# Weight blocks of a hybrid encoder layer, split two blocks ahead of their use instead of one

## The chip, the cores and the metric

The kernel runs on one core of one Trainium2 chip. The metric is device time in microseconds (us) of one execution, as the median of 3 runs. The core has a matrix engine (TensorE, PE in the profile; its weight loads are listed apart as PEld), a vector engine (VectorE, DVE), a scalar engine (ScalarE, ACT), a general engine (GpSimd, POOL) and SyncE (SP), which here only issues DMAs. GpSimd issues DMAs too, in order with its own computations.

## The reference

One layer on 1024 tokens with 16 meta tokens ahead of them (L = 1040), D = 1024, all in float32:

```python
u = rms_norm(h, norm1_g) @ w_in                # w_in: 1024 x (mLSTM x, o, gates | q, k, v | two branch gates)
xc = silu(depthwise_conv(u.mx) + conv_b)       # per head: q_m, k_m = xc @ wq, xc @ wk;  v_m = u.mx
h_m = mlstm_bidirectional(q_m, k_m, v_m, gates)        # 4 heads, chunkwise recurrence, both directions
y_a = sigmoid(u.mo) * (rms_norm(h_m) * g + skip * xc)
y_b = neighbourhood_attention(rms_norm(u.q), rms_norm(u.k), u.v, rpb, meta_bias)   # 8 heads, 8x16 windows
mix = sigmoid(u.ga) * (y_a @ w_branch_a) + sigmoid(u.gb) * (y_b @ w_branch_b)
h = h + mix @ w_out
h = h + square(relu(rms_norm(h, norm2_g) @ w_ff1)) @ w_ff2
return h[:, 16:]
```

## The kernel before

**Products in three terms.** Nearly every large product is formed in a reduced-precision float type (`float32r`) in three terms: both factors are split into a high part and a low part (the rest), and high x high, high x low and low x high are summed in PSUM. `mm3` issues the three matmuls.

**Weight blocks.** `w_in` is cut into blocks of 128 output columns (128 x 1024 elements, 512 KB). 42 of them, and then the 8 blocks of `w_b` (128 x 512), go through one queue W, an instance of `Weights`, in the order of their use, which a table FILL sets: xm (input of the recurrence, blocks x), tmo (its output gate, m), q, k and v of the attention (n, v), the branch gates gb and ga (b, a). For block j, `high_to` takes a tile wh, and GpSimd's queue issues a DMA from `w_in` that rounds to the high part on its way (L161). `split_to` takes a tile wl, ACT writes the negated high part into it, and a second DMA from `w_in`, again on GpSimd's queue, adds the whole weight on top, which leaves the low part (L174):

```python
    def split_to(self, i):
        while self.n_lo <= min(i, len(self.srcs) - 1):
            self.high_to(j + 1)
            ...
            self.neg(l[:, 0:w], h[:, 0:w])
            self.nc.gpsimd.dma_start(l[:, 0:w], src, accum_op=OP.add)
```

A job that starts on block i calls `W.get(i)`, which splits up to block i + ahead. So with ahead = 1, when block i begins, the split of block i + 1 and the load of the high part of block i + 2 are asked for.

**g blocks.** `gemm_in` multiplies a weight block with the 8 normalised and split tiles of the input (xh, xl), in 2 or 3 blocks of columns; each is 24 matmuls into one of two PSUM banks (`gbank`, tile g), and then an evacuation by ACT or DVE (for gb, ACT's tanh). `gemm_in` is a generator, so that other work can go between its matmuls.

**What sets the order.** A `Filler` F holds these jobs. The recurrence of the four heads (`head_a` prepares q, k, v, the gates and masks of a head; `head_b` runs the 8 steps, forward and backward) is a chain of small matmuls (pi, pu, pn, 258 columns) between copies on ACT (nn, the state's high part Ch) and work on DVE. At points in it `F.share` puts in a share of the g matmuls. The next head's convolved inputs xc are split into xch and xcl at the end of the step loop (xcl by the same pair of negation and accumulating DMA, L239) and read by the matmuls pq. After the heads, the attention tiles are filled in the same way, then comes a stage of `w_b` (its g blocks are evacuated on DVE into gbq), beside which DVE and GpSimd form sums (ys, yq) for the products with the later weights, which the profile has from 850 us on. The instructions so written are ordered once more by a scheduler with its own model of time, engine by engine.

**Slots.** Weights, inputs, intermediate rows and masks share one pool of 44 tiles in SBUF, 128 x 1040 floats each (`slot`, NSLOT = 44). A tile is given out when its former user's last reader is done. Order on an engine and the giving of slots are fixed when the program is built.

Of the kernel before, what the change touches and what calls it, by code (L numbers as in the profile page):

```python
# [20 lines left out]
KC = 8  # L21
# [120 lines left out]
class Weights:  # L142
# [32 lines left out]
            self.parts[j][1] = l  # L175
            self.n_lo += 1

    def get(self, i, ahead=1):
        self.split_to(i + ahead)
        return self.parts.pop(i)  # L180


def build(tc, A, taps=None):
# [18 lines left out]
    def slot(name, dt=F32):  # L202
        return sp.tile([128, L], dt, name=name, tag="S")
# [16 lines left out]
    def copy(out, src, psum=False):  # L220
        n = free(out)
        k = load.pick([("V", 65 + n * (1.1 if psum else 0.55)), ("S", 90 + n * 0.85)])[0]
        if k == "V":
            V.tensor_copy(out, src)
        else:
            SC.copy(out, src)
# [99 lines left out]
    xh = [slot(f"xh{k}", F32R) for k in range(KC)]  # L326
    xl = [slot(f"xl{k}", F32R) for k in range(KC)]
# [71 lines left out]
    def gemm_block(wh, wl, n0, n, ks=KC, act=(xh, xl), off=0):  # L399
        ps = gbank()[:, 0:n]  # L400
        m = slice(n0 - off, n0 - off + n)
        for k in range(ks):
            c = slice(k * 128, (k + 1) * 128)
            mm3(ps, wh[:, c], wl[:, c], act[0][k][:, m], act[1][k][:, m], k == 0, k == ks - 1)
            yield 3 * n * 0.000422
        return ps
# [10 lines left out]
            ins = PE.matmul(ps, wl[:, k * 128:(k + 1) * 128], xh[k][:, m], start=False, stop=k == KC - 1)  # L417
        return ps, ins

    def gemm_in(wi, blocks, evac, ks=KC, act=(xh, xl), off=0, ahead=1):  # L420
        wh, wl = W.get(wi, ahead)
        for b, (n0, n) in enumerate(blocks):
            ps = yield from gemm_block(wh, wl, n0, n, ks, act, off)
            evac(b, n0, n, ps)
# [10 lines left out]
    def job_xm(j):  # L435
        xm[j] = slot(f"xm{j}")
        yield from gemm_in(w_mx[j], NB3, lambda b, n0, n, ps: copy(xm[j][:, n0:n0 + n], ps, True))
# [3 lines left out]
    def job_mo(j):  # L441
        tmo[j] = slot(f"tmo{j}")
        yield from gemm_in(w_mo[j], NB2, lambda b, n0, n, ps: SC.activation(
            tmo[j][:, n0 - NM:n0 - NM + n], ps, AF.Tanh, scale=0.5))
# [401 lines left out]
    def job_na(u):  # L846
        qf = slot(f"nqf{u}")
        yield from gemm_in(w_q[u], NB2, lambda b, n0, n, ps: copy(qf[:, n0 - NM:n0 - NM + n], ps, True),
                           ahead=1)
        kf = slot(f"nkf{u}")  # L850
        yield from gemm_in(w_k[u], NB3, lambda b, n0, n, ps: copy(kf[:, n0:n0 + n], ps, True),
                           ahead=1)
        NAT[u] = (qf, kf)

    def split_v(ps, out):
# [207 lines left out]
    def add_jobs(u):  # L1063
        for kind, j in FILL[u]:
            if kind == "x":
                F.add(f"xm{j}", job_xm(j), GX)
            elif kind == "m":
                F.add(f"mo{j}", job_mo(j), GE)
            elif kind == "b":
                F.add(f"gb{j}", job_gb(j), GE)  # L1070
            elif kind == "a":
                F.add(f"ga{j}", job_ga(j), GE)
            elif kind == "n":
                F.add(f"na{j}", job_na(j), GE + GX)
            else:
                F.add(f"nb{j}", job_nb(j), GX + 6)
# [655 lines left out]
```

## Time and profile before

| | before |
|---|---|
| median of 3 runs | 1669.43 us (1667.87 to 1671.40) |
| profiled execution | 1671.44 us, span 1669.7 us, mean granted clock 0.986 |
| PE / PEld / DVE busy | 1605.0 / 1358.5 / 1192.2 us (96% / 81% / 71%) |
| ACT / GpSimd busy | 806.1 / 420.8 us (48% / 25%) |

The span is the time from the first to the last instruction of the profiled execution; the rest of its time lies around it. The granted clock is the TensorE clock as a share of its full level (1.2 and 2.4 GHz are its two levels). Busy time of matmuls overlaps from one to the next: a 512-column matmul is recorded with 0.39 us, and the next begins 0.23 us after it. A number in square brackets at the end of a row is the idle time of the engine ahead of it in us, with what ended it. An operation is shown as out<-in by the names of the tiles; most instructions have line L137, the helper that records every operation, so they are told apart by their tiles.

### The profile page before, as it was taken

The numbers are of one execution on the slowest core, as the hardware profiler recorded it, in microseconds if no ns is written. First come the engines' busy times: TensorE is split into PE (matmuls) and PEld (weight loads), VectorE is DVE, ScalarE is ACT, GpSimd is POOL, SyncE is SP. The second block draws the span as 40 slices with busy tenths as digits, with TensorE's granted clock in tenths as the row PEclk, the third lists the DMA queues.
The fourth block names the chain that finished last, engine by engine and source line by source line (L and its number), as shares of the span: only waits on it lengthen the run. The fifth ranks groups of instructions, "written<-read, shape, count | busy, mean of one in ns | idle before, by whom it ended". The sixth has DMA issues, their size and how long they took to land.

```text
span 1669.7 us, 22510 instructions
## 1 busy us (share of the span) xinstructions
PE 1605.0 (96%) x8081; PEld 1358.5 (81%) x8081; DVE 1192.2 (71%) x2171; ACT 806.1 (48%) x1425; POOL 420.8 (25%) x476
## 2 busy tenths in 40 slices
PE   7998899999999999999899889799999999999999
PEld 7878789888989998888678667588888887888887
DVE  4537657474757776872589998986667685869597
ACT  5567566566747586753232335322222237353450
POOL 5010212122233313212466665640000000010100
PEclk9999999999999999999999999899999999999999
DMA  4352745546274534446735221033223558282833
GB/s 165 74 133 64 193 114 139 115 112 154 47 183 89 119 71 102 99 98 192 240 115 212 104 84 56 29 148 114 102 101 126 206 159 272 56 264 58 232 78 100
DMA packets 76399, 213.73 MB, mean 128 GB/s; under 512 B 11112, under 2 KB 21736, under 8 KB 76288
## 3 DMA queue, kind: packets, MB, share of 16 engines
q1 hardware_dynamic: 54976, 138.76, 23.7%
q0 software_dynamic: 21312, 73.54, 21.2%
q8 instruction: 64, 1.05, 0.3%
q14 instruction: 47, 0.39, 0.1%
HBM read 164.97 MB, written 38.76 MB: 122 GB/s over the span
## 4 chain that ended last, share of the span: by engine, by line
PE 71%; DVE 10%; issue 7%; DMA 7%; ACT 3%; POOL 2%; SPq 0%; POOLq 0%; DVEq 0%; ACTq 0%
PE pf L137 38%; PE g L137 23%; DMA wl<-w_in 3%; DVE ga L137 2%; PE po L137 2%; PE pp L137 1%; PE pt L137 1%; PE ps L137 1%; PE pi L137 1%; PE pn L137 1%; DMA gbd<-gbq 1%; PE pu L137 1%; DMA xcl<-xc 1%; DMA ra<-masks 1%; DMA wl<-w_b 1%
## 5 line engine op out<-in xcount | busy, mean ns | idle before, releaser
L137 PE MATMUL g<-xh,wh 128*128 128x512 f32 (+3 forms) x784 | 290.2, 370 | 7.4 <-DVE xm L137 3.9
L137 PE MATMUL g<-xh,wl 128*128 128x512 f32 (+3 forms) x784 | 287.6, 367 | 9.1 <-DMA wl<-w_in 9.1
L137 PE MATMUL g<-xl,wh 128*128 128x512 f32 (+3 forms) x784 | 286.9, 366 | 0.0
L137 PEld LDWEIGHTS g<-xh,wl 128*128 128x128 f32 x784 | 148.6, 190 | 28.8 <-DMA wl<-w_in 10.7
L137 PEld LDWEIGHTS g<-xh,wh 128*128 128x128 f32 x784 | 148.8, 190 | 25.7 <-DVE xm L137 4.2
L137 PEld LDWEIGHTS g<-xl,wh 128*128 128x128 f32 x784 | 148.8, 190 | 17.0
L137 DVE TENSOR_TENSOR acc<-acc,pf 128x512 f32<-128x512 f32 x96 | 64.0, 680 | 39.6 <-PE pf L137 34.6
L174 POOL DMA_DIRECT2D wl<-w_in x42 | 38.5, 917 | 140.6 <-ACT wl L137 75.5
L137 DVE CUSTOM_DVE_ANT_0 P<-ps,bt 128x400 f32<-128x400 f32 x64 | 36.0, 570 | 42.2 <-PE pp L137 22.3
L137 ACT COPY pu<-pf 128x512 f32<-128x512 f32 x20 | 11.7, 585 | 105.6 <-PE pf L137 105.6
L137 ACT ACTIVATE wl<-wh 128x1024 fp32r<-128x1024 f32 (+1 forms) x50 | 49.3, 988 | 26.5 <-PE g L137 12.7
L137 DVE SCALAR_TENSOR_TENSOR C<-C,decb,pu 128x258 f32<-128x258 f32 x52 | 23.6, 478 | 40.9 <-PE pu L137 40.6
L137 DVE SCALAR_TENSOR_TENSOR zq<-zq 128x512 f32<-128x512 f32 x64 | 47.4, 742 | 0.6
L137 ACT ACTIVATE P<-P,mn 128x400 f32<-128x400 f32 x64 | 40.3, 630 | 11.3 <-DVE mn L137 10.8
L137 DVE TENSOR_TENSOR pu<-pf,pu 128x512 f32<-128x512 f32 x40 | 27.3, 683 | 21.0 <-PE pf L137 21.0
L137 DVE TENSOR_TENSOR zq<-pf,pu 128x512 f32<-128x512 f32 x32 | 21.9, 684 | 25.4 <-PE pf L137 25.4
L161 POOL DMA_DIRECT2D wh<-w_in x42 | 28.0, 668 | 45.0 <-PE pk L137 14.5
L137 DVE TENSOR_SCALAR P<-P,sm 128x384 f32<-128x384 f32 (+1 forms) x128 | 38.4, 363 | 0.9
L137 DVE TENSOR_TENSOR zq<-pf,sp 128x512 f32<-128x512 f32 x32 | 21.9, 685 | 22.6 <-PE pf L137 22.4
L137 DVE TENSOR_TENSOR ptl<-pp,pth 128x384 fp32r<-128x384 f32 x64 | 35.5, 554 | 2.8 <-ACT pth L137 2.1
L137 ACT CAST pth<-pp 128x512 fp32r<-128x512 f32 x60 | 34.0, 581 | 5.4 <-PE pp L137 5.2
L137 POOL COPY bt<-mbias 128x32 f32<-128x32 f32 x32 | 8.3, 260 | 111.9 <-DVE mn L137 111.8
(2414 smaller groups left out, 4989.8 us busy)
## 6 DMA issues: line engine op xcount, KB each, us to landing
wh<-w_in POOLq DMA_DIRECT2D x42, 512.0 KB, 5.6
wl<-w_in POOLq DMA_DIRECT2D x42, 512.0 KB, 5.6
z2d<-zq SPq DMA_DIRECT2D x32, 512.0 KB, 3.7
zr<-z2d SPq DMA_DIRECT2D x32, 512.0 KB, 5.0
w2r<-w_ff SPq DMA_DIRECT2D x32, 512.0 KB, 13.0
bt<-rpbd SPq DMA_DIRECT2D x256, 32.0 KB, 2.8
xcl<-xc POOLq DMA_DIRECT2D x8, 520.0 KB, 5.0
ra<-rowd SPq DMA_DIRECT2D x8, 512.0 KB, 4.2
```

What stands on the lines that cost most here:

```text
L137: return fn(out, *a, **k)
L161: self.nc.gpsimd.dma_start(h[:, 0:src.shape[-1]], src)
L174: self.nc.gpsimd.dma_start(l[:, 0:w], src, accum_op=OP.add)
```

## The change

`ahead` is 2 instead of 1, in `Weights.get`, in `gemm_in` and in the two calls of `job_na`. When block i begins, the split of block i + 2 and the load of the high part of block i + 3 are asked for.

```diff
-    def get(self, i, ahead=1):
+    def get(self, i, ahead=2):
         self.split_to(i + ahead)
         return self.parts.pop(i)
...
-    def gemm_in(wi, blocks, evac, ks=KC, act=(xh, xl), off=0, ahead=1):
+    def gemm_in(wi, blocks, evac, ks=KC, act=(xh, xl), off=0, ahead=2):
         wh, wl = W.get(wi, ahead)
...
         yield from gemm_in(w_q[u], NB2, lambda b, n0, n, ps: copy(qf[:, n0 - NM:n0 - NM + n], ps, True),
-                           ahead=1)
+                           ahead=2)
...
         yield from gemm_in(w_k[u], NB3, lambda b, n0, n, ps: copy(kf[:, n0:n0 + n], ps, True),
-                           ahead=1)
+                           ahead=2)
```

Every engine has the same instructions as before; the order differs, nearly all of it in the stretch of the weight blocks. The numbers behind a tile's name count the tiles as the program takes them, the digits in the name are its own index.

On GpSimd's queue at the end of head 0 and the start of head 1: wl7 is the low part of block 7 of W, wh8 and wh9 the high parts of blocks 8 and 9, rv and rsh finish a head, kl1 is the low part of head 1's k, ra are the mask rows. Before:

```order
L137 TENSOR_SCALAR rv_1742<-ssh_1268 128x2 [waits Activation_49]
L137 TENSOR_TENSOR rsh_1269<-rv_1742,mhalf_108 128x2 [waits Pool_49]
L137 TENSOR_SCALAR rv_1745<-ssh_1268 128x2 [waits Activation_49]
L137 TENSOR_TENSOR rsh_1269<-rv_1745,mhalf_108 128x2 [waits Pool_49]
L137 TENSOR_SCALAR rv_1882<-ssh_1268 128x2 [waits DVE_49,Activation_49]
L137 TENSOR_TENSOR rsh_1269<-rv_1882,mhalf_108 128x2 [waits Pool_49]
L137 TENSOR_SCALAR rv_1885<-ssh_1268 128x2 [waits DVE_49,Activation_49]
L137 TENSOR_TENSOR rsh_1269<-rv_1885,mhalf_108 128x2 [waits Pool_49]
L161 DMA wh8_2123<-w_in 128x1024 [waits DMASW6_49,PE_49]
L239 DMA kl1_2096<-kf1_2032 128x1040 [waits DMASW7_49,DMASW2_49,Activation_49]
L651 DMA ra10_2100<-masks 128x1024 [waits DMAHW2_49,DMASW0_49]
L174 DMA wl7_2125<-w_in 128x1024 [waits DMASW1_49,Activation_49]
```

And after:

```order
L137 TENSOR_TENSOR rsh_1274<-rv_1747,mhalf_108 128x2 [waits Pool_49]
L174 DMA wl7_1926<-w_in 128x1024 [waits DMASW7_49,Activation_49]
L137 TENSOR_SCALAR mbias_706<-mbias_706 128x128
L137 TENSOR_SCALAR rv_1750<-ssh_1273 128x2 [waits Activation_49]
L137 TENSOR_TENSOR rsh_1274<-rv_1750,mhalf_108 128x2 [waits Pool_49]
L137 TENSOR_SCALAR rv_1887<-ssh_1273 128x2 [waits DVE_49,Activation_49]
L137 TENSOR_TENSOR rsh_1274<-rv_1887,mhalf_108 128x2 [waits Pool_49]
L137 TENSOR_SCALAR rv_1890<-ssh_1273 128x2 [waits DVE_49,Activation_49]
L137 TENSOR_TENSOR rsh_1274<-rv_1890,mhalf_108 128x2 [waits Pool_49]
L161 DMA wh9_2128<-w_in 128x1024 [waits DMASW0_49,DVE_49,PE_49]
L239 DMA kl1_2101<-kf1_2037 128x1040 [waits DMASW6_49,DMASW1_49,Activation_49]
L651 DMA ra10_2105<-masks 128x1024 [waits DMAHW5_49,DMAHW3_49,DMASW2_49]
```

The accumulation of wl7 has gone from behind the mask load ra10 to ahead of mbias and of most of the 128x2 operations; the loads of wh are one block further on.

On ACT at the end of head 2: gb3 is the fourth gate tile, evacuated in two halves, nn and Ch belong to the steps of the recurrence, xch7 and xcl7 are the next head's convolved input. Before:

```order
L137 ACTIVATE xt7_4059<-xc7_4055 128x1040
L137 ACTIVATE gb3_3952<-g_3958 128x512
L137 ACTIVATE jk_3962,ssh_3452<-ht20_3432 128x256
L137 ACTIVATE jk_3964,ssh_3452<-ht20_3432 128x256
L137 ACTIVATE nn_4016<-pi_3980,tm_699 128x258
L137 CAST Ch_3998<-C_3996 128x258
L137 ACTIVATE nn_4018<-pi_3984,tm_699 128x258
L137 ACTIVATE jk_3966,ssh_3452<-ht21_3433 128x256
L137 CAST Ch_4004<-C_4002 128x258
L137 CAST xch7_4135<-xc7_4055 128x1040
L137 ACTIVATE xcl7_4136<-xc7_4055 128x1040
L137 ACTIVATE gb3_3952<-g_4101 128x512
```

And after:

```order
L137 CAST Ch_4009<-C_4007 128x258
L137 ACTIVATE nn_4021<-pi_3985,tm_699 128x258
L137 ACTIVATE nn_4023<-pi_3989,tm_699 128x258
L137 ACTIVATE jk_3971,ssh_3457<-ht21_3438 128x256
L137 ACTIVATE jk_3973,ssh_3457<-ht21_3438 128x256
L137 ACTIVATE nn_4083<-pi_4067,tm_699 128x258
L137 ACTIVATE nn_4085<-pi_4071,tm_699 128x258
L137 ACTIVATE xt7_4064<-xc7_4060 128x1040
L137 ACTIVATE gb3_3957<-g_3963 128x512
L137 ACTIVATE gb3_3957<-g_4106 128x512
L137 CAST xch7_4140<-xc7_4060 128x1040
L137 ACTIVATE xcl7_4141<-xc7_4060 128x1040
```

The two evacuations of gb3 were ten rows apart; now they stand together, behind the nn of the following step and xt7. The pair of gb1 at the end of head 1 has moved in the same way, to behind two nn and two Ch. On TensorE, 18 small matmuls of the recurrence now stand between gb1's second g block and the next g block, and 46 between gb3's and the next; before it was none in both places.

On DVE in the w_b stage: gbq20 to gbq31 are evacuations of g blocks of `w_b`, ys and yq the sums. Before:

```order
L137 TENSOR_TENSOR yq10_9203<-yq00_9158,yq10_9203 128x1024
L137 SCALAR_TENSOR_TENSOR gbq20_9166<-gbq20_9166,g_9304 128x512
L137 TENSOR_TENSOR ys11_9335<-yq11_9205,yq13_9209 128x1024
L137 SCALAR_TENSOR_TENSOR gbq21_9168<-gbq21_9168,g_9319 128x512
L137 TENSOR_TENSOR yq11_9205<-yq01_9160,yq11_9205 128x1024
L137 TENSOR_TENSOR yq02_9162<-yq02_9162,yq00_9158 128x1024
L137 TENSOR_TENSOR ys11l_9343<-ys11_9335,ys11h_9342 128x1024
L137 SCALAR_TENSOR_TENSOR gbq30_9254<-gbq30_9254,g_9349 128x512
L137 SCALAR_TENSOR_TENSOR gbq31_9256<-gbq31_9256,g_9363 128x512
L137 TENSOR_TENSOR ys20l_9380<-yq00_9158,ys20h_9379 128x1024
```

And after:

```order
L137 SCALAR_TENSOR_TENSOR gbq20_9171<-gbq20_9171,g_9307 128x512
L137 TENSOR_TENSOR ys10_9337<-yq10_9208,yq12_9212 128x1024
L137 TENSOR_TENSOR yq10_9208<-yq00_9163,yq10_9208 128x1024
L137 SCALAR_TENSOR_TENSOR gbq21_9173<-gbq21_9173,g_9322 128x512
L137 TENSOR_TENSOR ys11_9338<-yq11_9210,yq13_9214 128x1024
L137 TENSOR_TENSOR yq11_9210<-yq01_9165,yq11_9210 128x1024
L137 SCALAR_TENSOR_TENSOR gbq30_9259<-gbq30_9259,g_9349 128x512
L137 TENSOR_TENSOR ys11l_9346<-ys11_9338,ys11h_9345 128x1024
L137 TENSOR_TENSOR yq02_9167<-yq02_9167,yq00_9163 128x1024
L137 SCALAR_TENSOR_TENSOR gbq31_9261<-gbq31_9261,g_9363 128x512
L137 TENSOR_TENSOR ys20l_9380<-yq00_9163,ys20h_9379 128x1024
L137 SCALAR_TENSOR_TENSOR gbq30_9259<-gbq30_9259,g_9397 128x512
```

The evacuation into gbq30 stood behind yq02 and ys11l and now stands ahead of both; gbq31 stays behind them.

## Rows read from the trace of the kernel before

**Rows 1.** Totals of the page, busy us, share and count per engine.

```profile
PE 1605.0 (96%) x8081; PEld 1358.5 (81%) x8081; DVE 1192.2 (71%) x2171; ACT 806.1 (48%) x1425; POOL 420.8 (25%) x476
```

**Rows 2.** Stages: stretch, length, PE, PEld, DVE, ACT, POOL (count), clock, DMA, GB/s.

```profile
57.00:300.00 243.00, 225.72 (x1333) 202.41 (x1332) 148.94 (x402) 149.22 (x316) 38.88 (x56) 0.98 0.51 122
300.00:757.00 457.00, 451.19 (x2639) 405.35 (x2639) 319.23 (x900) 302.96 (x626) 111.33 (x217) 1.00 0.46 105
757.00:850.00 93.00, 86.50 (x365) 67.55 (x363) 45.49 (x46) 32.61 (x46) 39.06 (x29) 0.96 0.71 216
850.00:1000.00 150.00, 139.63 (x567) 109.75 (x566) 140.10 (x128) 49.19 (x68) 99.76 (x53) 0.95 0.35 125
```

**Rows 3.** Matmuls reading tile wl: min/median/max ns, first to last start, forms.

```profile
L137 PE MATMUL g<-xh,wl x784: 276/390/665, 57.8 to 787.0; 128*128 128x512 f32 x112, 128*128 128x256 f32 x28, 128*128 128x384 f32 x28, 128*128 128x400 f32 x28
```

**Rows 4.** Waits of PE, 57 to 757 us: releaser, sum us, count, longest.

```profile
PE g L137 <- DMA wl<-w_in: 9.1, 5, 3.9
...
PE pi L137 <- ACT Ch L137: 3.3, 4, 2.1
```

**Rows 5.** Waits of PE, 757 to 850 us.

```profile
PE g L137 <- DVE gbq L137: 6.0, 5, 3.1
```

**Rows 6.** Timeline, 170 to 208 us: start, us, engine, line, operation.

```profile
170.58 0.29 POOL L137 TENSOR_SCALAR mbias<-mbias 128x128 f32<-128x128 f32 x1
...
190.11 1.05 ACT L137 ACTIVATE wl<-wh 128x1024 fp32r<-128x1024 f32 x1
...
192.27 1.15 POOL L174 DMA_DIRECT2D wl<-w_in  x1
...
207.39 0.50 PE L137 MATMUL g<-xh,wl 128*128 128x512 f32 x1 [3.88 <-DMA wl<-w_in]
```

**Rows 7.** DMA issues, 185 to 212 us: count, KB each, us to landing.

```profile
wl<-w_in POOLq DMA_DIRECT2D x1, 512.0 KB, 15.1
```

**Rows 8.** DMA issues over the whole span, page part 6.

```profile
wl<-w_in POOLq DMA_DIRECT2D x42, 512.0 KB, 5.6
```

**Rows 9.** A stretch behind 207 us, columns as in group 2.

```profile
208.00:212.00 4.00, 4.00 (x12) 3.16 (x11) 1.03 (x4) 1.86 (x7) 0.00 (x0) 0.58 0.90 317
```

**Rows 10.** Timeline, GpSimd's queue.

```profile
187.65 0.62 POOL L161 DMA_DIRECT2D wh<-w_in  x1 [7.34 <-PE pk L137]
```

**Rows 11.** Timeline, end of head 2.

```profile
357.22 0.92 POOL L239 DMA_DIRECT2D xcl<-xc  x1 [3.42 <-DVE ht L137]
...
360.04 0.48 ACT L137 ACTIVATE nn<-pi,tm 128x258 f32<-128x258 f32 x1 [0.23 <-PE pi L137]
...
370.92 0.39 PE L137 MATMUL pq<-xcl,wqk 128*128 128x512 f32 x1
```

**Rows 12.** Timeline, end of head 1, PE and ACT.

```profile
254.18 0.40 PE L137 MATMUL g<-xh,wh 128*128 128x512 f32 x1
...
259.05 0.40 ACT L137 CAST Ch<-C 128x258 fp32r<-128x258 f32 x1
```

**Rows 13.** Timeline, PE before 355 us.

```profile
353.80 0.28 PE L137 MATMUL pn<-vh,sml 128*128 128x258 f32 x1
...
353.92 0.39 PE L137 MATMUL g<-xh,wh 128*128 128x512 f32 x1
...
354.61 0.39 PE L137 MATMUL g<-xh,wh 128*128 128x512 f32 x1
```

**Rows 14.** Timeline, w_b stage.

```profile
818.76 1.22 DVE L137 TENSOR_TENSOR ys<-yq,yq 128x1024 f32<-128x1024 f32 x1
...
828.86 3.22 POOL L137 TENSOR_TENSOR yq<-ys,yq 128x1024 f32<-128x1024 f32 x1 [2.96 <-DVE yq L137]
...
829.77 3.38 DVE L137 TENSOR_TENSOR ys11l<-ys,ys11h 128x1024 fp32r<-128x1024 f32 x1
...
833.08 1.27 DVE L137 SCALAR_TENSOR_TENSOR gbq<-gbq,g 128x512 f32<-128x512 f32 x2
...
833.81 0.79 PE L137 MATMUL g<-yb0h,wh 128*128 128x512 f32 x1 [3.12 <-DVE gbq L137]
```

## The prediction

> **What bounds the kernel now.** I read the totals first [rows 1]. TensorE (PE) is busy 1605.0 of 1669.7 us; its weight loads, 81%, overlap its matmuls, and VectorE (DVE) has 71%, ScalarE (ACT) 48%, GpSimd 25%. The table by stage [rows 2] says where PE is not full. The weight blocks are used from 57.8 us [rows 3] to about 850. In that time, 57 to 300 us has PE busy 225.72 of 243.00 (17.3 free), 300 to 757 has 451.19 of 457.00 (5.8 free), and 757 to 850 has 86.50 of 93.00 (6.5 free). So the change can win little more than 29.6 us, under 2%, and only where its own wait is the one that ends last. From 850 to 1000 the busiest engine is DVE, 140.10 of 150.00.
>
> The list of PE's waits over the first two of these stages [rows 4] has the change's target in its first line: matmuls that read a low part wl wait for its landing 5 times, 9.1 us in all, the longest 3.9. The next line is of another kind, the rows pi of the recurrence that wait for ACT's copy of its state Ch. In the w_b stage [rows 5] the largest wait, 6.0 us, is for gbq, DVE's evacuation of PSUM, and not for a weight.
>
> **What the change does, step by step.** *The lead.* A block of w_in lasts (787.0 - 57.8) / 42 = 17.4 us on average [rows 3], so high and low parts are asked for about that much earlier. The longest wait shows that this is enough. The negated copy of that block stood on ACT at 190.11, and GpSimd issued its accumulating DMA at 192.27; PE took the block at 207.39 after 3.88 idle [rows 6]. That DMA took 15.1 us to land [rows 7], where the median of all 42 is 5.6 [rows 8]: two loads of masks went out around it. In the changed order on GpSimd's queue the same DMA (wl7) stands ahead of mbias, which ran at 170.58 [rows 6]. So it is issued at about 170, and even with 15.1 us it lands some 20 us before 207. The other four waits are 5.2 us together, each far shorter than a block. Term A: -9.1 us, bounds 0 (another input is late at the same places) and -9.1.
>
> *The clock.* After that 3.88 us wait the granted clock fell: 0.58 over 208 to 212 us, with 12 matmuls [rows 9]. At 0.23 us from one 512-column matmul to the next at the full level (three in 0.69 [rows 13]), 4 us hold 17.4; the 5.4 that are missing are 1.2 us. Without the wait this stretch should stay at the full level. Term B: -1.2, bounds 0 and -1.2.
>
> *The work.* Nothing is added: 50 negations on ACT, 50 copies and 50 accumulations on GpSimd's queue stay, each only earlier on its queue; SP's queue issues none of them. ACT has half its time free and GpSimd three quarters [rows 1], so a negation of 1.05 us [rows 6] that comes earlier costs PE nothing by itself. Behind wl7 there now stand the 128x2 operations that finish a head, and those wait only for its issue, 1.15 us [rows 6]. In wl7's old place, between the two mask loads, now goes wl8, whose block is used one block later, so that 15 us for its landing do no harm.
>
> *The slots.* This is the cost. One more high and one more low part live among the 44 slots. That slots are short already is seen where a load of wh, which reads only an input, waits 7.34 us for matmuls of pk [rows 10]: it waits for the last reader of the tile that held its slot. The weights now take such slots first, and others wait. The clearest places in the order are two pairs of evacuations on ACT. The first of gb3 stood ten rows ahead of the second; now both stand together, behind the last nn of the step, which ran at 360.04, and xt [rows 11]. The g blocks have two PSUM banks, so PE can't start the block after gb3 before the first is evacuated. By the old times that is 360.04 + 0.48 (nn) + 1.05 (xt, as large as a negation) + 0.60 (gb) = 362.2, against 354.61, where PE started it [rows 13]: 7.6 us. gb1 is alike: its pair now stands behind a pair of Ch whose second ran at 259.05; 259.05 + 0.40 + 0.60 = 260.1, against 254.18 for the next block [rows 12]: 5.9 us. Together 13.5 us if nothing else ran there. But the changed order puts 18 and 46 small matmuls of the recurrence into these two holes; at 0.12 us from one to the next [rows 13] these are 7.7 us. Left are 5.8. The recurrence itself is quicker when no g matmuls stand in it, so a part of that goes too. The nearest row for a step that lacks cover is PE's wait for Ch, 2.1 us at the longest and 3.3 in 4 [rows 4]. Term C: +3.0, nearest to that row; bounds 0 and +13.5.
>
> *The w_b stage.* PE's worst wait there, 3.12 us, ends with an evacuation of gbq at 833.08, which stood on DVE behind ys11l of 3.38 us, two adds and another evacuation [rows 14]. In the changed order the first of this pair of evacuations (gbq30) stands ahead of ys11l and one of the adds, but the second (gbq31) still behind both. So about half of that wait goes. Term D: -1.5, bounds 0 and -6.2 (nearly all of the stage's 6.5 free us). Against it: the adds of that stage take 1.22 us when GpSimd computes nothing, and 3.38 beside GpSimd's own add of 3.22 [rows 14]; so DVE has little to give there, and what PE gains may be waited for after 850, where DVE is 93% busy [rows 2]. The Trainium skill ("SBUF — State Buffer", SBUF: two separate sides) says that GpSimd and DVE operations on two SBUF inputs hold a shared pair of ports as an exclusive lock; the trace agrees with its 1.22 against 3.38. By that rule the adds of both engines follow one another whatever the order, and term D would be nothing.
>
> Sum: -9.1 - 1.2 + 3.0 - 1.5 = -8.8 us. The profiled execution took 1671.44 us, of which the span is 1669.7; that gives 1662.6. It lies 2.0 above the median of the runs, 1669.43, so I predict 1660.6, rounded 1661. (With term D nothing, by the skill's rule, it would be 1662.)
>
> **Rivals.** *Slots starve the recurrence, slower.* Place: heads 1 and 2, around 254 to 260 and 354 to 371 us, and the start of the next head. The full 13.5 us are paid, since the small matmuls in the holes are themselves steps that wait for ACT and DVE, and the second convolved half is late too. The DMA of its low part was issued at 357.22, and with the 5.6 us of such a DMA [rows 8] it was there at 362.8 for a matmul pq at 370.92 [rows 11], 8.1 us of room. The order now has its two copies xch and xcl behind gb3's second evacuation: 362.2 + 0.6 + 1.05 + 1.05 (copies as large as a negation) + 5.6 = 370.5. PE, which starts its next block at 362.2 and has 48 g matmuls of 0.23 us before pq, comes there at 373.2: 2.7 us of room. But both copies take slots as well, and a wait for a slot as long as that of wh, 7.34 us [rows 10], makes it 377.8, so PE waits 4.6. Price 13.5 + 4.6 = 18.1, less A, B and D (11.8): +6.3, so 1676. It decides from 11.8 us of new waits on. For it: loads of wh already wait for readers [rows 10], and PE is at 98.7% from 300 to 757 [rows 2], where there is mostly loss to make. Against it: with the step's g matmuls gone from between them, the 64 small ones can run closer together, and then the pairs of evacuations come earlier than by the old times. The Trainium skill speaks for it: "Perfetto Trace Analysis", Optimization Strategy, says that gaps which repeat on the engine that should be full can mean too little SBUF to get the next tile ready. The trace shows that for GpSimd's loads (7.34 us), not yet for PE.
>
> *The wait is hidden anyway, no change.* The g matmuls that wait for wl fill the time of the recurrence; if that sets a head's length, PE's 9.1 us come back as waits for Ch and its like. For it: in 57 to 300 us PE has 17.3 us free, and wl is only a part. Against it: PE takes its matmuls in order, and behind each late one the next stood queued [rows 9]. Time: A and B come back, C and D cancel, 1669 give or take 3.
>
> *The change doesn't do what it says*: wl gets no slot, and the split runs as late as before. The order speaks against it, since every wl that waited has moved ahead by a block; I count it into the case before.
>
> **How the numbers follow.** Chances: forecast 0.56, no change 0.22, slots 0.22. A difference under 0.2% (3.3 us) can't be told from none. The forecast's own range is 1653 (A, B and all of D, no C: -16.5) to 1666 (C at its 5.8, A and B, no D: -4.5, rounded up). The range for 8 in 10 reaches on through the no-change case to the slot case: 1652 to 1676.
>
> **What would show it.** In the profile after: PE's list of waits from 57 to 757 us without wl, or with under 1.5 us of it (A); a granted clock near 1.00 around 208 us (B); PE free for 1 to 3 us each near 255 and 355 us, ending with gb or Ch (C); gbq30 ahead of ys11l and a wait shorter than 3.12 (D); PE's free time from 57 to 300 us down from 17.3 to about 10. I'd be wrong if waits of several us appear for gb, xcl, nsp or vh, or if wl is gone from the list and the stage is as long as before.

## The result and the profile after

The change makes the kernel slower: 1683.29 us (median of 4 runs, 1681.07 to 1686.29) against 1670.41 us, a ratio of 1.0089 with a 95% interval of 1.0072 to 1.0106, so +12.9 us. The forecast was -8.8 us, and the range ended at 1676. The profiled execution took 1686.29 us, 3.0 above its median; that of before lay 1.0 above its own. The totals of the page after:

```profile
span 1684.5 us, 22521 instructions
...
PE 1612.2 (96%) x8081; PEld 1364.8 (81%) x8081; DVE 1195.0 (71%) x2171; ACT 805.0 (48%) x1425; POOL 421.3 (25%) x476
```

The counts are those of [rows 1]: no work was added; PE's busy time grew by 7.2 us, since more of its matmuls ran at the low clock (below). The same stages as in [rows 2]:

```profile
57.00:300.00 243.00, 227.06 (x1317) 203.36 (x1315) 148.02 (x400) 149.13 (x312) 37.87 (x56) 0.96 0.53 125
300.00:757.00 457.00, 447.94 (x2595) 402.46 (x2596) 312.43 (x882) 297.42 (x617) 111.32 (x217) 0.99 0.46 105
757.00:850.00 93.00, 87.75 (x396) 71.43 (x395) 45.34 (x58) 30.51 (x47) 32.63 (x26) 0.97 0.64 196
850.00:1000.00 150.00, 135.15 (x545) 105.37 (x543) 139.67 (x122) 51.21 (x67) 100.64 (x47) 0.95 0.34 121
```

In the same 457 us from 300 on, PE issued 44 matmuls fewer than before. PE's waits from 57 to 757 us, which answer to [rows 4]; first a line of the kernel before that is not shown there, then after:

```profile
PE g L137 <- ACT xm L137: 1.7, 3, 1.1
```

```profile
PE g L137 <- ACT xm L137: 5.8, 3, 2.3
PE pi L137 <- ACT Ch L137: 5.7, 7, 2.3
PE g L137 <- DVE xm L137: 3.9, 1, 3.9
PE pr L137 <- ACT nsp L137: 3.5, 3, 2.2
```

The line for wl is gone, as forecast. In its place stand longer waits for ACT's evacuations of xm and for Ch, and new ones for nsp. The one wait for DVE's xm (3.9 us) is the same in both kernels; in the full list of before it is the second line, ahead of the one for Ch that the prediction called the next.

**Where the time went.** Both programs issue the same matmuls on PE. Where the set of those already issued is the same in both, the start times of the next one can be subtracted. That gives how far a kernel's profiled execution is behind the one of before (us), by place in the kernel before:

```
place (us of before)  170   222   301   365   402   433   534   568   719   805   857    end
after                +1.4  +1.5  +4.7  +8.5  +6.4 +12.7 +17.0 +16.0 +10.3  +9.6 +15.0 +14.9
lead_heads           +1.9  +1.5  +3.2  +6.1  +4.0 +10.5 +11.3 +10.8 +10.0  +9.6 +14.6 +15.4
lead_late            +2.3  -1.1  -0.9  -0.9  -2.5  -2.5  -2.5  -3.5  -9.2  -9.1  -8.6  -9.5
lead_w_b             +0.7  -2.9  -2.8  -2.8  -4.4  -4.4  -4.4  -4.8  -5.9  -6.8  -2.3  -3.8
slots42              +1.5  +7.0  +9.2 +13.2 +11.2 +17.6 +24.4 +24.1 +26.9 +26.6 +35.4 +35.0
slots43              +1.7  +1.4  +2.2  +2.4  +0.4  +1.3  +1.7  +0.7  +0.2  +0.5  +4.3  +6.5
heads_nsp            +0.9  +2.4  +5.4  +8.2  +6.1  +6.3  +6.5  +6.2  +7.2  +6.7  +9.4  +9.9
heads_extra          +2.9  -0.7  +2.6  +3.4  +1.5  +8.0  +9.2  +9.1  +9.4  +8.8 +11.2 +12.4
heads_low2           +0.8  -3.1  -1.4  -0.7  -2.5  -1.6  +0.8  +0.6  -0.3  -0.2  -0.7  -1.2
heads_high3          +1.3  +4.4  +7.6  +6.9  +4.8  +5.8  +6.1  +5.9  +6.6  +6.6  +6.2  +3.9
full_extra3          +0.6  -2.4  -1.9  -0.1  -2.0  -1.9  -0.3  -1.2  -6.9  -7.7  -4.4  -5.4
best_f               -0.8  -5.7  -4.7  -3.9  -5.7  -5.6  -5.7  -6.7 -12.3 -12.4 -11.8 -12.2
```

(The lower lines are the experiments below; a few places are the nearest point that a kernel has.) A single execution is good to some 3 us in such a column: lead_late and lead_w_b have before's own order up to 560 us, and still are 3.4 and 3.6 us ahead between 170 and 222, where before's wait of 3.88 [rows 6] was 0 and 1.43 in them. Read so, the changed kernel falls back by 11.3 us up to 433, by 4.3 more to 534, wins 6.7 from 534 to 719, and loses 5.4 from 805 to 857. The two largest single steps up to 433 us are 6.3 us between 402 and 433, and 4.4 us between 300 and 304 (from +2.6 to +7.0).

**The place from 402 to 433 us.** The first attention head pair squares k and q in blocks (ACT writes a tile nsp), and PE sums them (pr). In the kernel before, ACT filled the last three of these tiles within 3 us, ahead of PE:

```profile
423.18 0.42 ACT L137 ACTIVATE nsp<-nkf 128x256 fp32r<-128x256 f32 x1
424.50 0.53 ACT L137 ACTIVATE nsp<-nkf 128x384 fp32r<-128x384 f32 x1
426.18 0.52 ACT L137 ACTIVATE nsp<-nkf 128x400 fp32r<-128x400 f32 x1
```

After, ACT fills one only when PE is through with the one before, ACT first and then PE:

```profile
436.19 0.42 ACT L137 ACTIVATE nsp<-nkf 128x256 fp32r<-128x256 f32 x1
436.63 1.28 ACT L137 ACT_TABLE_LOAD   x1
437.92 1.15 ACT L137 ACTIVATE nsq<-nsq,eps 128x1024 f32<-128x1024 f32 x1
...
439.23 0.52 ACT L137 ACTIVATE nsp<-nkf 128x384 fp32r<-128x384 f32 x1
...
441.31 0.54 ACT L137 ACTIVATE nsp<-nkf 128x400 fp32r<-128x400 f32 x1
```

```profile
437.09 0.48 PE L137 MATMUL pr<-nsp,ones_r 128*128 128x256 f32 x2
439.81 0.44 PE L137 MATMUL pr<-nsp,ones_r 128*128 128x384 f32 x1 [2.24 <-ACT nsp L137]
...
441.91 0.70 PE L137 MATMUL pr<-nsp,ones_r 128*128 128x400 f32 x1 [1.00 <-ACT nsp L137]
```

The addresses in the built programs say why. Before, the five nsp tiles lay in three slots (two, two and one). After, four of them follow one another in a single slot. The order on ACT is built around that: a table load and nsq, which before stood behind all three, now stand between the first and the second, and most of the wait of 2.24 us is their time. That is the shortage of slots, at a place that the prediction named only among the things that would prove it wrong. The two waits are 3.2 us; the rest of the 6.3 that are lost here is about what the clock costs, at the lower of its two levels for nearly all of the 7 us from 441 on (clock is the third number from the end; before it was 1.00 over this work). It is as low from 304 us on, around the longest wait for xm (2.28):

```profile
441.00:448.00 7.00, 5.99 (x24) 5.69 (x25) 3.84 (x12) 4.36 (x9) 0.00 (x0) 0.51 0.00 0
304.00:311.00 7.00, 5.03 (x15) 4.97 (x16) 3.39 (x8) 5.77 (x19) 0.00 (x0) 0.54 0.43 120
```

**The start of head 1.** The accumulation of wl7 went out at 171.63 instead of 192.27. PE waits for other things now:

```profile
170.99 0.45 PE L137 MATMUL g<-xh,wh 128*128 128x400 f32 x1 [2.03 <-ACT xm L137]
...
196.90 0.45 PE L137 MATMUL g<-xh,wh 128*128 128x400 f32 x1 [1.47 <-ACT xm L137]
...
212.37 0.58 PE L137 MATMUL pi<-Ch,qh 128*128 128x258 f32 x1 [2.25 <-ACT Ch L137]
```

Ahead of xm on ACT now stands the copy for xcl, which before ran ahead of five small copies (Ch and nn) of the recurrence, and now runs behind them; the negation stood there before too, for the block ahead of this one:

```profile
168.27 1.07 ACT L137 ACTIVATE xcl<-xc 128x1040 fp32r<-128x1040 f32 x1
...
169.64 1.04 ACT L137 ACTIVATE wl<-wh 128x1024 fp32r<-128x1024 f32 x1
170.59 0.73 ACT L137 COPY xm<-g 128x256 f32<-128x256 f32 x2
```

The built programs say why here too. Before, this xcl (xcl3) had the slot of gb0, whose last reader, a DMA, went out at 150.1 us, and its copy ran at 164.47. After, it has the slot of vl01, a tile of head 0, and its copy waits for the last matmul that reads vl01:

```profile
167.91 0.32 PE L137 MATMUL pn<-vl,smh 128*128 128x258 f32 x1
```

**The place from 300 to 304 us.** The longest wait for xm has another cause. In both programs ACT's evacuation of xm stands behind eight operations on a mask row ra of head 2, which wait for the DMA of the mask. Before, and then after:

```profile
298.49 2.45 ACT L137 ACTIVATE ra<-ra,tm 128x128 f32<-128x128 f32 x8 [7.76 <-DMA ra<-masks]
300.84 0.35 ACT L137 COPY xm<-g 128x256 f32<-128x256 f32 x1
```

```profile
303.22 2.44 ACT L137 ACTIVATE ra<-ra,tm 128x128 f32<-128x128 f32 x8 [10.33 <-DMA ra<-masks]
305.58 0.35 ACT L137 COPY xm<-g 128x256 f32<-128x256 f32 x1
...
305.97 0.70 PE L137 MATMUL g<-xh,wh 128*128 128x400 f32 x1 [2.28 <-ACT xm L137]
```

This mask row has another slot as well: before that of xm5, last read at 278.7 us, so that its first load went out at 278.97; after that of xch4, last read at 285.8, so that it went out at 286.20. The Ch of the wait at 212.37 now stands behind head 1's first mask row (in the slot of xch3, last read at 188.8; before in that of xch2, at 186.4). But the later slot is not the whole cause: in full_extra3 (below) the load of head 2's mask row goes out at 281.65, also late, and that place loses nothing. No run separates the slot from the other DMAs that run beside the mask's.

### The profile page after: what moved, and what is told of

It is laid out like the page before. It is cut to its first block, busy times and chain, and to the rows that moved or that the text cites. A ratio compares the mean times of both kernels' runs of the same rounds, so it can differ in the third digit from the quotient of the medians.

```text
span 1684.5 us, 22521 instructions
## 1 busy us (share of the span) xinstructions
PE 1612.2 (96%) x8081; PEld 1364.8 (81%) x8081; DVE 1195.0 (71%) x2171; ACT 805.0 (48%) x1425; POOL 421.3 (25%) x476
## 5 line engine op out<-in xcount | busy, mean ns | idle before, releaser
L137 PE MATMUL g<-xh,wh 128*128 128x512 f32 (+3 forms) x784 | 291.9, 372 | 11.5 <-ACT xm L137 5.8
L137 PEld LDWEIGHTS g<-xl,wh 128*128 128x128 f32 x784 | 150.1, 191 | 16.6
L137 ACT ACTIVATE nn<-pi,tm 128x258 f32<-128x258 f32 x60 | 27.0, 473 | 23.4 <-PE pi L137 23.3
L137 ACT CAST pth<-pp 128x512 fp32r<-128x512 f32 x60 | 33.9, 580 | 3.3 <-PE pp L137 2.9
```

Of the source, the lines that this page charges most:

```text
L137: return fn(out, *a, **k)
```

## Experiments

Medians are compared with the kernel before in the same comparison. A kernel's name is that of its line in the table above.

**Which blocks.** The lead of two is given to some blocks only. In the order on PE, each such part moves only its own stretch and little behind it.

```diff
     def get(self, i, ahead=1):
+        if i + 2 < 27:              # lead_heads; 27 <= i + 2 < 42: lead_late; i + 2 >= 42: lead_w_b
+            ahead = 2
         self.split_to(i + ahead)
```

> Lead of two only for blocks 2 to 26 of W (the heads and the first attention blocks), one for all others. Theory (the loss is made in the heads): the profile after is 16.0 us behind at the block after index 26, about 567 us, so this part alone costs +14 to +16 us against the kernel before, 1684 to 1686 us. Rival (the loss is spread, and the w_b stage carries half of it): +5 to +8 us.

1687.45 us, ratio 1.0103 (1.0085 to 1.0120), +16.8, slightly more than expected: this part alone loses even more than the whole change. But by its column only 10.8 us of it are there by 568 us. Another 5.0 come between 805 and 857, where every engine has its order of before. There DVE's add ya40l waited for a DMA and ran 3.35 us, and PE waited 4.6 us for the gbq behind it (longest before: 3.1):

```profile
821.22 3.35 DVE L137 TENSOR_TENSOR ya40l<-yq,ya40h 128x1024 fp32r<-128x1024 f32 x1 [2.63 <-DMA gbd<-gbq]
824.49 0.68 DVE L137 SCALAR_TENSOR_TENSOR gbq<-gbq,g 128x512 f32<-128x512 f32 x1
...
825.22 0.79 PE L137 MATMUL g<-yb0h,wh 128*128 128x512 f32 x1 [4.58 <-DVE gbq L137]
```

So most of the loss is made in the heads, and a part in a stage that the edit leaves as it was; why is not shown.

> Lead of two only for blocks 27 to 41 of W (attention tiles, 567 to 757 us). Theory: the three waits for wl that the kernel before has there (blocks 29, 33, 37; 4.1 us with no new wait in the profile after) go: -4 to -6 us, about 1665. Rival (slots cost everywhere, also here): 0 to +3 us.

1661.93 us, 0.9946 (0.9934 to 0.9959), -8.7, more than expected: the waits that went were 4.1 us. No wait for wl is left after 555 us, and none came in its place. This part of the change is a gain by itself.

> Lead of two only for the 8 blocks of w_b (index 42 to 49). Theory: PE reads its weights sooner but DVE and GpSimd bind that stage, and the new order makes PE wait for gbq and then for wa0c: +3 to +5 us (the profile after loses 4.6 from 720 us on). The prediction's term D, as rival: -1.5 us.

1671.76 us, 1.0010 (0.9997 to 1.0023): no difference that can be told from none. Of the theory's +3 to +5 its interval (-0.5 to +3.8) holds the lower end; term D's -1.5 lies outside. PE's waits from 757 to 880 us:

```profile
PE g L137 <- DVE gbq L137: 6.0, 2, 3.8
PE pf L137 <- DVE wa0c L137: 3.6, 1, 3.6
```

In the profile the first half of the stage gains (-5.9 to -6.8 by 805, and -11.5 by 834), and the second half gives it back by 857: PE comes sooner to work of DVE that is no sooner done.

**How many slots.** The kernel before, lead of one, with 42 and with 43 slots (`NSLOT = 42`, `NSLOT = 43`).

> The kernel before, lead of one, with 42 slots in place of 44: as many slots gone as the longer lead takes. Theory (the heads' loss is a shortage of slots): from 57 to 567 us it falls behind by 8 to 16 us as the changed kernel does, with late evacuations of xm and a wait for nsp; whole time +8 to +20. Rival (the earlier negations and loads stand in front of other work in the queues, slots have nothing to do with it): less than 4 us lost from 57 to 567.

1704.49 us, 1.0195 (1.0173 to 1.0217), +33.9, and 24.1 behind by 568 us: the direction that was expected, but far above its ranges. Two slots less, with no lead changed, lose 6.4 from 402 to 433 us where the changed kernel loses 6.3. The same tiles follow the same ones in their slots: four nsp in one, xcl3 behind vl01, the first mask rows of heads 1 and 2 behind xch3 and xch4. The same wait stands in the list of 57 to 757 us:

```profile
PE g L137 <- DMA wl<-w_in: 13.6, 6, 4.6
...
PE pr L137 <- ACT nsp L137: 3.2, 2, 2.2
```

Here the weights wait too, since they get no slots ahead of others.

> The kernel before, lead of one, with 43 slots. Theory (a slot's worth in the heads is what heads_high3 lost): +4 to +10 us, nsp tiles in two slots. Rival (heads_high3 lost it by its earlier loads, one slot can be spared): under +2.

1681.92 us, 1.0090 (1.0068 to 1.0112), +13.3, more than expected, and in another place. Up to 805 us its profile is level with before (+0.5); it loses in the w_b stage and after (its profiled execution is 3.9 us under its median). In the heads, one slot can be spared. So the rival holds there, and the price of a slot is not even: 1.7 us by 534 us for the first, 22.7 more for the second.

**Which slots.** Two of the five nsp tiles of the first head pair come from a tile of their own, in 4 KB of each partition that the head stage leaves free (heads_nsp), or the high parts of four blocks do (heads_extra), both with the lead of lead_heads.

```diff
+    extra = msp.enter_context(tc.tile_pool(name="ex", bufs=1))
...
-                pr = slot(f"nsp{u}{n0}", F32R)
+                if u == 0 and (f_ is qf and n0 == 512 or f_ is kf and n0 == 256):       # heads_nsp
+                    pr = extra.tile([128, L], F32R, name=f"nsp{u}{n0}", tag="X")
+                else:
+                    pr = slot(f"nsp{u}{n0}", F32R)
...
-            h = self.slot(f"wh{j}", F32R)
+            if j in (3, 7, 11, 15):                                                      # heads_extra
+                h = self.extra.tile([128, L], F32R, name=f"wh{j}", tag="X")
+            else:
+                h = self.slot(f"wh{j}", F32R)
```

> Lead of two in the heads as in lead_heads (1687), and two of the five nsp tiles of the first attention head pair come from one tile of their own beside the 44 slots. Theory: in the changed kernel four nsp tiles share one slot, so that each square on ACT waits for the matmul pr that reads the tile before it; PE waits 3.2 us for nsp around 440 us, its clock falls, 6.6 us are lost between 402 and 434 us of the kernel before. With a second tile that place costs under 2 us: about 1681. Rival (nsp is late because ACT has other work first): no change, 1687.

1679.76 us, 1.0066 (1.0047 to 1.0084): +11.1, so 5.8 us less than lead_heads, of 6.6 expected. From 402 to 433 us its profile loses 0.2 in place of 6.5, and nsp is gone from PE's waits. This is the clearest test of the cause: one tile for one place took that place's loss away.

> Lead of two in the heads, and the high parts of blocks 3, 7, 11 and 15 have one tile of their own beside the 44 slots (free for others from block 16 on, where the nsp tiles come). Theory: the 3 to 6 us that lead_heads is behind by 365 us shrink to 0 to 2, the place of nsp stays: 1682 to 1685. Rival (order, not slots): 1687.

1683.07 us, 1.0084 (1.0064 to 1.0103): +14.4, as expected. By 365 us it is at +3.4 in place of +6.1 (expected 0 to 2), by 402 at +1.5 in place of +4.0, though PE began 3 us late (below); the place of nsp stays, as expected (+6.5).

**Which of the two extra tiles.** `split_to` asks for the high part of the block behind the one that it splits.

```diff
-            self.high_to(j + 1)
+            self.high_to(j if j < 27 else j + 1)            # heads_low2, with the lead of lead_heads
+            self.high_to(j + 2 if j + 1 < 27 else j + 1)    # heads_high3, with a lead of one
```

> Low parts two ahead in the heads, high parts two ahead as before instead of three: one slot more than before instead of two, all negations and accumulations as early as in lead_heads. Theory (slots): about half of the loss, 1675 to 1681, and nsp in two slots. Rival (early negations and accumulations in the queues): all of it, 1687.

1669.41 us, 1.0002 (0.9992 to 1.0012): nothing lost. The negations and accumulations, as early as in lead_heads, cost nothing; the rival is out. The theory's half of the loss is not there either.

> High parts three ahead in the heads, low parts one ahead as before: also one slot more than before, but no negation or accumulation earlier. Theory (slots): about half of the loss, 1675 to 1681, although nothing is gained, the waits for wl stay. Rival (early negations): no loss, 1670.

1675.66 us, 1.0038 (1.0024 to 1.0052): +7.0, with no negation earlier. The time fits the theory, but slots43 shows that one slot alone costs the heads nothing. What its profile has more than before is a wait for kl, whose accumulating DMA stands behind a load of wh on GpSimd's queue (3.3 us in 57 to 555; before 0.3):

```profile
PE ps L137 <- DMA kl<-kf: 3.3, 2, 1.8
```

That load waits 8.60 us for its slot in this profile, 7.34 before [rows 10]. But that made kl's DMA only 1.0 us later (191.64, before 190.62), which then took 10.8 us to land instead of 8.8, and lead_late, with before's order there, waits 0.9 us for kl too. So what costs the 7 us is not shown.

**The whole change with a tile more.** All 50 blocks two ahead, and the tile serves blocks 3, 7, 11, 15 and then nsp (full_extra); without block 3 (full_extra2); with a mask row of head 0 as its first user (full_extra3).

> The whole change (lead of two for all 50 blocks) with one tile more beside the 44 slots while the heads run: it takes the high parts of blocks 3, 7, 11 and 15, and then two of the nsp tiles. Theory (slots): the parts measured alone add up, heads_extra +14.4, less 7.7 for nsp, lead_late -8.7, lead_w_b +1.2: -0.8 us, 1665 to 1671, so that the 13 us are gone. Rival (the order on the queues costs the larger part): 1678 or more.

1671.46 us, 1.0015 (1.0003 to 1.0028), +2.3, just above the expected range; PE began 3.4 us late.

> The whole change with one tile more in the heads, as full_extra, but the tile takes the high parts of blocks 7, 11 and 15 only (and then two nsp tiles). In full_extra its first load, of block 3, went out at 1.25 us, before the input rows, and PE began 3.4 us later than in the kernel before. Theory (slots make the loss): that 3.4 us goes too, 1666 to 1669, no slower than the kernel before. Rival (something of the change beside slots costs 2 us or more): 1671 or more.

1670.42 us, 1.0012 (1.0001 to 1.0023), +1.8: a miss. The edit did not reach its aim: the scheduler sent the first load into the free tile at once again, ahead of the input's rows, and PE began 2.9 us late.

```profile
1.27 0.72 POOL L164 DMA_DIRECT2D wh<-w_in  x1 [0.44 <-issue]
```

> The whole change with the tile more in the heads, which now serves first a mask row of head 0, then the high parts of blocks 7, 11 and 15, then two nsp tiles, so that no load into it can go out at the start (full_extra2's still did, and PE began 2.9 us late). Theory (slots make the loss): 1665 to 1668.5, no slower than the kernel before. Rival (the start was not on the path): 1670 as full_extra2.

1666.84 us, 0.9990 (0.9980 to 1.0001), -1.8, as expected. With one tile more, the change loses nothing: 14.7 us better than without. In its column it is level with before in the heads, keeps the gain from 534 to 719, and gives part of it back in the w_b stage. Against full_extra2 it is 3.6 us quicker, about what its earlier start gives.

**A version that beats both.** best_c: the low parts of all of w_in two ahead, the third high part from block 27 on, w_b one ahead. best_a: the same with the tile of full_extra; best_a2 with that of full_extra2. best_b: the lead of lead_late and the tile. best_f: low parts two ahead up to block 19, one ahead to 26, the full lead for 27 to 41; best_e: the same with the tile of full_extra3.

```diff
+        if i + 2 < 20 or 27 <= i + 2 < 42:                   # best_f
+            ahead = 2
...
-            self.high_to(j + 1)
+            self.high_to(j if j < 20 else j + 1)
```

> Lead of two for the low parts of all blocks of w_in, the third high part only from block 27 on, lead of one for w_b, and the tile more in the heads as in full_extra. Theory: lead_late's -8.7, and 1 to 3 us more from the slot in the heads: 1657 to 1661. Rival (the heads are set by the recurrence, a slot more gives nothing): 1661 to 1663.

1665.28 us, 0.9980 (0.9969 to 0.9992), -3.9: a miss, behind the rival's range too. PE began 3.0 us late.

> Lead of two only for blocks 27 to 41, lead of one in the heads and for w_b, and the tile more in the heads. Theory: if a slot less costs 7 us in the heads (heads_high3), one more gives 1 to 5 us: 1657 to 1661. Rival (44 slots are enough at a lead of one): 1662 as lead_late.

1678.54 us, 1.0052 (1.0033 to 1.0070), +9.3: a miss, 18 us slower than lead_late, and the strongest word against "more slots are faster". PE began 2.6 us late; and with a lead of one and a tile more, it waits for weights:

```profile
PE g L137 <- DMA wl<-w_in: 11.2, 4, 4.8
```

The tile changed which slot each later tile got. The load of block 18 went out at 370.1, 10.7 us later than in lead_late, and the accumulation of block 17 behind it at 371.3 instead of 361.0; at a lead of one that was too late.

> Lead of two for the low parts of all blocks of w_in, the third high part only from block 27 on, lead of one for w_b, 44 slots and no tile more. Theory: heads_low2 (+0.7) and lead_late (-8.7) add up: 1660 to 1664. Rival (the gain of lead_late and the cost in the heads are not independent): 1666 or more.

1666.51 us, 0.9979 (0.9966 to 0.9992), -2.7: a miss, and in the rival's range; 8.5 us are lost between 433 and 534.

> As best_a (low parts two ahead in all of w_in, third high part only from block 27 on, lead of one for w_b, a tile more in the heads), the tile without block 3. Theory: best_a's 1665 less the 3.0 us at its start: 1661 to 1663. Rival (starting sooner only meets the same inputs of the recurrence): 1664 to 1666.

1665.54 us, 0.9984 (0.9972 to 0.9996), -3.1: a miss, and in the rival's range, with a late start again.

> 44 slots. Low parts two ahead for blocks up to 19, one ahead for 20 to 26 and for w_b, and the full lead of two for blocks 27 to 41. Theory: the loss of best_c from 433 to 534 us (8.5 us in its profile) came with the lead of blocks 20 to 26, which the first attention tiles and the end of head 3 share; it goes, and 1658 to 1662 is left. Rival (it came from the earlier blocks): 1665 as best_c.

1660.47 us, 0.9954 (0.9936 to 0.9971), -8.2: as expected. The loss from 433 to 534 came with the lead of blocks 20 to 26, and is gone. It is the lowest median here, though not apart from lead_late.

> As best_f, with the tile more in the heads that full_extra3 has. Theory: best_a2's profile was 7.6 us ahead of its own start at 402 us; with no late start and without the loss from 433 to 534 us: 1655 to 1660. Rival (a tile more gives nothing at a lead that the slots already hold): as best_f.

1666.36 us, 0.9989 (0.9977 to 1.0000), -2.3: a miss. The tile cost 6 us against best_f; in its profile PE waits up to 4.5 us for xm between 193 and 209 us; what made that late is not shown.

## Why the prediction was wrong

**Term A (-9.1) held for less than half.** The lead was enough: no wait for wl is left. But the prediction took each wait of one execution as a gain. The three late ones (4.1 us) were, and for more than their own time: the profile wins 6.7 from 534 to 719, as lead_late's does, which is -8.7 by its runs. The two early ones (5.0) were not: from 170 to 222 us the changed kernel is where it was (+1.4, +1.5), with xm 2.03 and 1.47 and Ch 2.25 in their place. That looks like the rival "hidden anyway", but the rows say otherwise for xm 2.03 and Ch 2.25: they end behind a copy and a mask row that got later slots. heads_low2, with the low parts as early, wins 3.9 there (+0.8 to -3.1). Yet lead_late, with no lead there, wins 3.4: the 3.88 of [rows 6] was 0 and 1.43 in other executions of the same order. So what these two waits were worth can't be told from one execution each.

**Term B (-1.2) had the wrong sign.** From 208 to 212 us the granted clock is 1.00 now, as forecast, but 0.76 from 212 to 219, behind the wait for Ch; the other new waits brought 0.51 and 0.54 after nsp and xm. Over 57 to 300 us it fell from 0.98 to 0.96, over 300 to 757 from 1.00 to 0.99. The sum counted the clock only where a wait goes, not where one comes.

**Term C (+3.0) is the step that failed.** The mechanism, slots, was named; its place and size were not. The two places that the prediction worked out, behind gb1 and gb3, cost 0 and 1.0 us (a wait for ht at 364.43): the small matmuls there ran in the hole, as its own "against it" said. The loss came at places that it did not price: four nsp tiles in one slot (6.3 us), a late mask row ahead of xm (4.4 us between 300 and 304), and a late copy of xcl ahead of xm. Taken alone, the lead in the heads costs 16.8 us against +3.0, net of whatever term A gave there; by its column 10.8 of it are in the stretch that the term was about, inside the bound of 13.5, and the 5.0 behind 805 us, where that kernel's order is the old one, are in no term. The slot rival ("1676") had the right sign, for other rows. (The forecast's own range ends at 1666; by its terms, 1669.4 less 4.5, that end is 1665. Nothing hangs on it.)

**Term D (-1.5).** lead_w_b measured +1.2 (-0.5 to +3.8), so nothing. The argument against it was right: PE gains up to 834 us (lead_w_b -11.5 there) and DVE takes it back by 857. In the profile after, its adds beside GpSimd's take 3 us each, and the evacuation gbq that PE waits for stands behind two of them:

```profile
839.60 3.12 DVE L137 TENSOR_TENSOR ys11l<-ys,ys11h 128x1024 fp32r<-128x1024 f32 x1
842.64 3.39 DVE L137 TENSOR_TENSOR yq<-yq,yq 128x1024 f32<-128x1024 f32 x1
845.95 0.67 DVE L137 SCALAR_TENSOR_TENSOR gbq<-gbq,g 128x512 f32<-128x512 f32 x1
```

```profile
839.73 0.50 PE L137 MATMUL g<-yb0h,wh 128*128 128x512 f32 x1 [2.91 <-DVE gbq L137]
846.68 0.50 PE L137 MATMUL g<-yb0h,wh 128*128 128x512 f32 x1 [2.34 <-DVE gbq L137]
...
866.32 0.74 PE L137 MATMUL pf<-ys30h,wa0c 128*128 128x512 f32 x2 [3.60 <-DVE wa0c L137]
```

Before there was one such wait of 3.12 [rows 14]; now there are three. The Trainium skill's rule ("SBUF — State Buffer", SBUF: two separate sides), an exclusive lock between GpSimd and DVE, forecast that term D comes to nothing, and it did; no run here took GpSimd's adds away, so the lock itself is not shown.

The parts, +16.8, -8.7 and +1.2, add up to 9.3, and the whole measured 12.9; the intervals of the three (about 3, 2 and 2 us to each side) can hold that. That a slot is what the heads lacked is shown for the nsp place by heads_nsp, and for the whole by full_extra3 and slots42 together; against it stands that a tile more also deals all later slots anew, by which best_b and best_e lost. Early negations as a cause are out by heads_low2. For the late xcl and the mask rows the slots are read from the programs, and no run changes one of them alone. The 4.3 us that the changed kernel loses from 433 to 534, heads_high3's 7 us, the 6 us of best_e, and the losses behind 805 us in lead_heads and slots43 stay open.

## What to carry to other kernels

A longer lead is paid in the buffers of whoever shares the pool: list, by address, which tiles follow one another in one slot after the change, above all short chains of write, read, write between two engines. Where a pool is nearly full, the price of one tile more is a step, not a slope (here 1.7, then 22.7 us by 534 us), and the same tile can help one order and hurt another (full_extra3, best_b). Ask stage by stage where the wait to be removed is really the last one, and give the lead only there: the late third of the blocks had all of the gain here.

## What the runs showed of the hardware

Short idle times of PE cost about double here: the waits of 2.24 and 1.00 us for nsp came with 7 us at a granted clock of 0.51, and the place lost 6.3 us by its matched matmuls; the wait of 2.28 us for xm came with 7 us at 0.54, and that place lost 4.4. With a 512 KB DMA issued at 1.27 us, ahead of the input's rows, PE's first matmul was 2.9 us later (full_extra2), and that profile ends 4.1 us behind the one of full_extra3, which has no such early load.
